# Softmax over 32768 columns on one core: eight equal column pieces per tile in place of five, and a finer cut of the last tile

## Chip, cores and metric

One core of a Trainium2 chip. The metric is the device time of one execution in microseconds, of the slowest core (here the only one). Executions of one kernel mostly agree within 0.3%. A run counts as slow when it lies more than 1.5% above the fastest of the same kernel; verdicts use the other runs, called fast here.

## The reference

```python
batch, seq, vocab = 16, 256, 32768          # logits: float32, temperature: 1.0
scaled = logits / temperature
scaled = scaled - scaled.max(axis=-1, keepdims=True)
exp_scaled = np.exp(scaled)
return exp_scaled / exp_scaled.sum(axis=-1, keepdims=True)
```

4096 rows of 32768 floats: 537 MB to read and 537 MB to write.

## The kernel before

Each row is cut into two halves that lie on neighbouring partitions, so there are 8192 half rows, 64 tiles of 128 half rows by 16384 columns (8.39 MB each). There are three tile buffers, of 64 KB per partition each. A tile is loaded, turned into probabilities in place, and stored from the same buffer. Loads go through the queue of the sync engine (SP), middle stores through that of ScalarE.

```python
_PIECES = (4096, 4096, 4096, 2048, 2048)
_ON_DVE = (4096, 4096, 2048, 0, 0)
_END = 4096                       # first and last tile: four pieces
_END_ON_DVE = 2560

def normalise(t):
    ...
    for k in range(K):            # one piece after the other
        nc.vector.tensor_reduce(out=nm[:, k:k+1], in_=xc, axis=X, op=A.max, negate=True)
        nc.scalar.activation(out=xc, in_=xc, func=Exp, bias=nm[:, k:k+1],
                             scale=inv_t, accum_out=ssum[:, k:k+1])
        if t == 1 and k == 0:
            store(0, 0, W)
    # max over pieces and over the two halves of a row; small exp `ee`; sum; reciprocal; factor f
    ...
    for k in range(K):            # scale: on_dve[k] columns on VectorE, the rest on ScalarE
        ...
        if t == G - 1:
            store(t, a, c)
    if 0 < t < G - 1:
        store(t, 0, W)

for t in range(_BUFS):
    load(t)
for t in range(G):
    normalise(t)
    if t and t + _BUFS - 1 < G:
        load(t + _BUFS - 1)       # waits until the store of tile t-1 is over
```

Each piece has a max of its own, so ScalarE can start its exp while VectorE looks at the next piece; the factors f put the pieces on one scale at the end.

## Time and profile before

| | kernel before |
|---|---|
| median of its first 3 runs | 2494.04 us (2493.56 to 2495.87) |
| span of the profiled run | 2496.7 us |
| VectorE (DVE) / ScalarE (ACT) busy | 63% / 55% |
| moved over the span | 430 GB/s |
| a middle tile: first max to store issue | 28.05 us |

In lines of a timeline the columns are the start in us, the length in us, engine, line of the kernel, operation, output <- input, shapes and the number of instructions that are merged; brackets give idle time before it and what ended that. In a table of stretches they are the stretch, its length, the busy time of each engine with its instruction count, the granted TensorE clock, the mean share of the 16 DMA engines, and GB/s. For the last two a packet is counted whole in the stretch in which it starts, so stretches of a few us show jumps that are not there. From the timeline of the kernel before:

```profile
1044.95 0.34 ACTq L70 DMA_DIRECT2D out_dram<-x  x1
1050.72 0.33 SPq L62 DMA_DIRECT2D x<-in_logits_dram  x1
```

The second line is the next load, issued once the store before this one has landed, 5.8 us later.

### The profile page before, as it was taken

What the parts mean: (1) busy time and instruction counts of PE and PEld (TensorE: products, weight loads), DVE (VectorE), ACT (ScalarE), POOL (GpSimd) and SP (SyncE); (2) the same over time, 40 slices, a digit from 0 to 9 for tenths busy, and PEclk for the clock granted to TensorE, in tenths of its full rate; (3) what the DMA queues carried; (4) which work ended last, traced back from release to release, by engine and by line L of the source; (5) the groups of instructions that cost most, each with busy time, mean ns of one, the idle gap of its engine ahead of it and who ended that gap; (6) DMA issues with size and microseconds to landing.
All of it is one profiled execution on the core that took longest, in us unless ns stands there. A gap on an engine that the chain in (4) does not pass through costs nothing.

```text
span 2496.7 us, 2616 instructions
## 1 busy us (share of the span) xinstructions
DVE 1575.6 (63%) x1216; ACT 1367.8 (55%) x895; POOL 0.2 (0%) x4
## 2 busy tenths in 40 slices
DVE  6576665766657656576565665656657566565665
ACT  6464654645546455464554645546455464554655
POOL 0000000000000000000000000000000000000000
DMA  9999999999999999999999999999999999999998
GB/s 419 436 429 430 433 437 436 435 437 426 434 434 437 433 426 435 434 436 423 433 433 433 435 425 436 436 433 425 435 422 436 421 437 436 421 436 422 436 429 380
DMA packets 19748, 1073.91 MB, mean 430 GB/s; under 512 B 2192, under 2 KB 2192, under 8 KB 2192
## 3 DMA queue, kind: packets, MB, share of 16 engines
q1 hardware_dynamic: 10800, 553.65, 51.4%
q10 hardware_dynamic: 8928, 520.10, 48.4%
q14 instruction: 20, 0.16, 0.0%
HBM read 536.87 MB, written 536.87 MB: 430 GB/s over the span
## 4 chain that ended last, share of the span: by engine, by line
DMA 73%; DVE 16%; ACT 9%; another core or an unknown queue 2%; issue 0%; SPq 0%; DVEq 0%; ACTq 0%
DMA x<-in_logits_dram 37%; DMA out_dram<-x 36%; DVE nm L101 12%; ACT x L108 7%; DVE x L140 3%; ACT x L144 2%; DVE f L136 0%; ACT ee L121 0%; DVE rS L135 0%; DVE Sh L80 0%; DVE ttj L124 0%; DVE Sh L77 0%; SPq L62 0%; DVEq L189 0%
## 5 line engine op out<-in xcount | busy, mean ns | idle before, releaser
L101 DVE TENSOR_REDUCE nm<-x 128x1 f32<-128x4096 f32 x318 | 1117.5, 3579 | 683.8 <-DMA x<-in_logits_dram 683.8
L108 ACT ACTIVATE x<-x,nm 128x4096 f32<-128x4096 f32 x318 | 965.4, 3036 | 1025.3 <-DVE nm L101 1025.3
L144 ACT ACTIVATE x<-x,f 128x2048 f32<-128x2048 f32 (+1 forms) x194 | 370.9, 1975 | 74.0 <-DVE f L136 74.0
L140 DVE TENSOR_SCALAR x<-x,f 128x4096 f32<-128x4096 f32 (+2 forms) x194 | 372.2, 1975 | 2.5 <-DVE f L136 0.2
L124 DVE CUSTOM_DVE_ANT_0 ttj<-ee,ssum 128x5 f32<-128x5 f32 (+1 forms) x64 | 10.6, 166 | 196.7 <-ACT ee L121 196.7
L108 ACT ACTIVATION_READ_ACCUMULATOR x<-x,nm 128x1 f32 x318 | 59.2, 186 | 0.0
L121 ACT ACTIVATE ee<-nm,nMh 128x5 f32<-128x5 f32 (+1 forms) x64 | 18.1, 284 | 0.0
L136 DVE TENSOR_SCALAR f<-ee,rS 128x5 f32<-128x5 f32 (+1 forms) x64 | 14.8, 231 | 2.2
L135 DVE RECIPROCAL rS<-Sh 128x1 f32<-128x1 f32 x64 | 10.5, 164 | 2.2
L80 DVE TENSOR_TENSOR Sh<-Sh 128x1 f32<-128x1 f32 x64 | 10.2, 159 | 2.2
L80 DVE TENSOR_TENSOR nMh<-nMh 128x1 f32<-128x1 f32 x64 | 10.2, 159 | 2.2
L119 DVE TENSOR_REDUCE nMh<-nm 128x1 f32<-128x5 f32 (+1 forms) x64 | 10.1, 158 | 2.2
L77 DVE STREAM_SHUFFLE Sh<-Sh 128x1 f32<-128x1 f32 x64 | 9.7, 151 | 0.0
L77 DVE STREAM_SHUFFLE nMh<-nMh 128x1 f32<-128x1 f32 x64 | 9.7, 151 | 0.0
L108 ACT ACT_TABLE_LOAD x1 | 1.3, 1283 | 8.1 <-DMA x<-in_logits_dram 8.1
L124 DVE DVE_READ_ACCUMULATOR2_ANT Sh<- 128x1 f32 x64 | 5.2, 82 | 0.0
L77 DVE LOAD_MASK_SELECT Sh<-Sh x64 | 0.9, 14 | 2.8
L77 DVE LOAD_MASK_SELECT nMh<-nMh x64 | 0.9, 14 | 2.8
L175 POOL MEMSET const-uint8-127<- 128x1 uint8 x1 | 0.1, 102 | 0.0
L175 POOL MEMSET const-bfloat16-1.0<- 128x1 bf16 x1 | 0.1, 101 | 0.0
L175 POOL MEMSET const-float32-0.0<- 128x1 f32 x1 | 0.1, 98 | 0.2 <-issue 0.2
L175 POOL MEMSET const-float32-1.0<- 128x1 f32 x1 | 0.1, 98 | 0.0
## 6 DMA issues: line engine op xcount, KB each, us to landing
x<-in_logits_dram SPq DMA_DIRECT2D x8, 2048.0 KB, 23.7
out_dram<-x SPq DMA_DIRECT2D x4, 2048.0 KB, 15.1
x<-in_logits_dram SPq DMA_DIRECT2D x62, 43.7
out_dram<-x ACTq DMA_DIRECT2D x62, 44.5
out_dram<-x SPq DMA_DIRECT2D x1, 29.4
```

Of the source, the lines that this page charges most:

```text
L77: nc.vector.stream_shuffle(out=v[:, j + 1 : j + 2], in_=v[:, j : j + 1], mask=mask)
L80: nc.vector.tensor_tensor(out=v[:, j + 1 : j + 2], in0=v[:, j : j + 1], in1=v[:, j + 1 : j + 2], op=op,)
L101: nc.vector.tensor_reduce(out=nm[:, k : k + 1], in_=xc, axis=X, op=A.max, negate=True)
L108: nc.scalar.activation(out=xc, in_=xc, func=Exp, bias=nm[:, k : k + 1], scale=inv_t, accum_out=ssum[:, k : k + 1],)
L119: nc.vector.tensor_reduce(out=nMh[:, 0:1], in_=nm, axis=X, op=A.min)
L121: nc.scalar.activation(out=ee, in_=nm, func=Exp, bias=nMh[:, n_rounds : n_rounds + 1], scale=-1.0)
L124: nc.vector.tensor_tensor_reduce(out=ttj, in0=ee, in1=ssum, scale=1.0, scalar=0.0, op0=A.mult, op1=A.add, accum_out=Sh[:, 0:1],)
L135: nc.vector.reciprocal(out=rS, in_=Sh[:, n_rounds : n_rounds + 1])
L136: nc.vector.tensor_scalar_mul(out=f, in0=ee, scalar1=rS)
L140: nc.vector.tensor_scalar_mul(out=xs[:, a:b], in0=xs[:, a:b], scalar1=f[:, k : k + 1])
L144: nc.scalar.activation(out=xs[:, b:c], in_=xs[:, b:c], func=Copy, scale=f[:, k : k + 1])
L175: nc = _bacc.Bacc("TRN2", target_bir_lowering=False, num_devices=1)
```

## The change

The intent: smaller, equal pieces let ScalarE keep up with VectorE, so that less is left after the last max and each store leaves earlier; in the last tile, smaller last pieces shorten the tail.

```diff
-_PIECES = (4096, 4096, 4096, 2048, 2048)
-_ON_DVE = (4096, 4096, 2048, 0, 0)
-_END = 4096
-_END_ON_DVE = 2560
+_PIECES = (2048, 2048, 2048, 2048, 2048, 2048, 2048, 2048)
+_ON_DVE = (2048, 2048, 2048, 2048, 2048, 0, 0, 0)
+_FIRST_PIECES = (4096, 4096, 4096, 4096)
+_FIRST_ON_DVE = (2560, 2560, 2560, 2560)
+_LAST_PIECES = (4096, 4096, 4096, 2048, 2048)
+_LAST_ON_DVE = (2560, 2560, 2560, 2048, 0)
 ...                              # load() and normalise() take their cut from cut(t)
-            if t == 1 and k == 0:
+            if t == 1 and k == 1:
                 store(0, 0, W)
```

More of the change, by code (lines that the diff above doesn't have):

```diff
@@ L10 @@
 _BUFS = 3
-_LOAD = 16384
-_PIECES = (4096, 4096, 4096, 2048, 2048)
-_ON_DVE = (4096, 4096, 2048, 0, 0)
-_END = 4096
-_END_ON_DVE = 2560
+_LOAD = (16384,)
+_PIECES = (2048, 2048, 2048, 2048, 2048, 2048, 2048, 2048)
[4 more added lines that the diff above has]
+_LAST_ON_DVE = (2560, 2560, 2560, 2048, 0)
 _SETS = 3
@@ L45 @@
     n_rounds = _SPLIT.bit_length() - 1
-    K = max(len(_PIECES), W // _END)
+    K = max(len(_FIRST_PIECES), len(_PIECES), len(_LAST_PIECES))
     pool = ctx.enter_context(tc.tile_pool(name="fixed", bufs=1))
@@ L57, with cut @@
     ]
+    def cut(t: int) -> tuple:
+        if t == 0:
+            return _FIRST_PIECES, _FIRST_ON_DVE, _FIRST_PIECES
+        if t == G - 1:
+            return _LAST_PIECES, _LAST_ON_DVE, _LAST_PIECES
+        return _PIECES, _ON_DVE, _LOAD
     def load(t: int) -> None:
-        n = _END if t in (0, G - 1) else _LOAD
-        for s in range(0, W, n):
+        s = 0
+        for n in cut(t)[2]:
             nc.sync.dma_start(
@@ L65, in load @@
             )
+            s += n
     def store(t: int, a: int, b: int) -> None:
@@ L88, in normalise @@
         xs = buf[t % _BUFS]
-        if t in (0, G - 1):
-            sizes = [_END] * (W // _END)
-            on_dve = [_END_ON_DVE] * len(sizes)
-        else:
-            sizes, on_dve = _PIECES, _ON_DVE
+        sizes, on_dve, _ = cut(t)
         K = len(sizes)
```

## The prediction

Its sum came to 0 in the middle, -1.1 us at the end for the DMA engines that don't set it and +1.6 for the one that does, +1 to +1.6 us in all, of which +1.0 was taken.

> **What bounds the kernel now.** I read the page of the kernel before from the top: the head, the 40 slices, the queues, the chain, the groups. Then the waits, the timeline of one middle tile and of the end, and a table of stretches over the end.
>
> ```profile
> DVE 1575.6 (63%) x1216; ACT 1367.8 (55%) x895; POOL 0.2 (0%) x4
> DMA  9999999999999999999999999999999999999998
> HBM read 536.87 MB, written 536.87 MB: 430 GB/s over the span
> DMA 73%; DVE 16%; ACT 9%; another core or an unknown queue 2%; issue 0%; SPq 0%; DVEq 0%; ACTq 0%
> L101 DVE TENSOR_REDUCE nm<-x 128x1 f32<-128x4096 f32 x318 | 1117.5, 3579 | 683.8 <-DMA x<-in_logits_dram 683.8
> ```
>
> Neither compute engine is the bound: VectorE is busy for 63% of the span and ScalarE for 55%, and VectorE's idle time (683.8 us) is waiting for loads. The transfers are at nine tenths or more in every slice but the last. Each tile is 128 rows of 16384 floats, 8.39 MB in and 8.39 MB out, and there are 64. The stretches confirm it:
>
> ```profile
> 800.00:1000.00 200.00, 125.79 (x106) 112.14 (x77) 0.00 (x0) 1.00 1.00 432
> 1000.00:1200.00 200.00, 128.56 (x100) 111.79 (x73) 0.00 (x0) 1.00 1.00 432
> ```
>
> The last two columns are the DMA share, 1.00, and 432 GB/s. At that rate a tile's 16.78 MB take 38.8 us, and that is the period at which tiles follow each other (first max at 1016.90, then at 1055.71). All 64 take 2485 us of the 2496.7 us span. So nothing that only shortens work on an engine can move the middle: the chain's 16% VectorE and 9% ScalarE are the way from a load to the store of the same tile, while another load and another store are in flight. What is left to win lies at the two ends, about 12 us together. The end:
>
> ```profile
> 2446.50:2469.70 23.20, 19.25 (x17) 16.15 (x11) 0.00 (x0) 1.00 1.00 429
> 2469.70:2471.70 2.00, 2.00 (x2) 2.00 (x2) 0.00 (x0) 1.00 0.15 66
> 2471.70:2491.40 19.70, 3.50 (x3) 3.42 (x3) 0.00 (x0) 1.00 1.00 425
> 2491.40:2495.10 3.70, 0.00 (x0) 0.00 (x0) 0.00 (x0) 1.00 0.06 27
> ```
>
> Three things are to be seen. Until 2469.7 the transfers are full. Then for 2.0 us they stand at a share of 0.15: the store before the last is drained on most of the 16 DMA engines and the last tile's first stored piece isn't there yet. From 2471.7 they are full again, and at 2491.4 fifteen engines are done. The share of 0.06 after it is one engine of sixteen (1/16 = 0.0625), which works alone at 27 GB/s for 3.7 us and sets the end. Individual DMA records agree: thirteen engines pause between 2469.7 and 2471.7, two go on to about 2472.2, and one still has two whole packets of the previous store to send, until 2475.6. That last one never pauses.
>
> [...] this trace holds 430 to 434[...]. [...] The queue part of this page has
>
> ```profile
> q14 instruction: 20, 0.16, 0.0%
> ```
>
> 20 packets, 0.16 MB, that is 8 KB each, for 2616 executed instructions: one packet for every 131. I read these as refills of the instruction streams. [...] here the max takes 4413 ns at 4096 and 2276 ns at 2048, so two halves cost 139 ns more than a whole, and the scaling 2350 and 1280, 210 ns more.
>
> **The change, part by part.** (a) Middle tiles, 62 of them, on VectorE: eight maxima of 2048 in place of three of 4096 and two of 2048: 8 x 2.276 - (3 x 4.413 + 2 x 2.276) = +0.42 us busy. Scaling: five of 2048 in place of two of 4096 and one of 2048: 5 x 1.280 - (2 x 2.350 + 1.280) = +0.42 us. Over 62 tiles +52 us: VectorE to about 1628 us. ScalarE: 8 x 1.985 - (3 x 3.708 + 2 x 1.985) = +0.79 us, and three more accumulator reads of 0.186; its three copies of 2048 stay. Over 62 tiles +83 us: ScalarE to about 1451 us. Both stay under 70% of the span, beside the transfers: zero on the path.
>
> (b) Way from load to store of a middle tile. This group's timeline shows it:
>
> ```profile
> 1016.90 17.46 DVE L101 TENSOR_REDUCE nm<-x 128x1 f32<-128x4096 f32 x5 [10.63 <-DMA x<-in_logits_dram]
> ...
> 1037.68 0.28 ACT L121 ACTIVATE ee<-nm,nMh 128x5 f32<-128x5 f32 x1
> ...
> 1039.06 5.81 DVE L140 TENSOR_SCALAR x<-x,f 128x4096 f32<-128x4096 f32 x3
> ```
>
> Now: the five maxima take 17.46 us with overlaps of about 0.07 each, and the small exp starts 20.78 us after the first, because ScalarE still has 4096-wide work queued. After: eight maxima at 2.21 are 17.7 us; ScalarE needs 1.98 per piece, less than 2.21, so it keeps up and the small exp starts about 2.0 later, at 19.7: 1.1 us earlier. The scaling then ends about 5 x 1.22 = 6.1 after its start in place of 5.81: 0.3 later. Net 0.8 us earlier per tile. In the middle this only makes a store wait longer in the queue: zero on the path.
>
> (c) The last two tiles, where VectorE does set the pace: the last tile's maxima start at 2446.58 with no idle time, straight after the scaling of the tile before, since its data had landed. The 0.8 us of tile 62 therefore moves the last tile forward. Inside the last tile, four maxima take 17.39 us and the small exp starts at 21.13 after the first; with 4096 three times and 2048 twice it is the old middle pattern, 20.78: 0.35 us earlier. The first stored piece has the same 2560 and 1536 columns. So the first of the last stores can be issued 1.1 us earlier, and the pause of 2.0 us shrinks to 0.9 for thirteen engines.
>
> (d) But the engine that ends last has no pause to shrink. Its end is the sum of its own transfers. Why it is behind: at the end 3.7 us, plus the 2.0 us pause that the others had, makes 5.7 us. An 8 KB packet at 27 GB/s takes 0.30 us, and 19 or 20 of them make 5.7 to 6.0 us. This is what it looks like if all refill packets run on this one engine; that is an estimate, not shown. The change adds instructions: VectorE 62 x (3 + 2) + 1 = 311; ScalarE 62 x (3 exps + 3 accumulator reads) + 2 = 374; one load and one store: some 687 in all, or 687/131 = 5.2 more packets. At 0.30 us each the last engine ends about 1.6 us later.
>
> (e) Start: tile 0 keeps its pieces. Its store is issued after the second piece of tile 1, which ends where the first 4096-wide one ended. Zero. Last stores in pieces of 1 MB: the same bytes, and the end is the straggler's last packet, so zero to within the 0.6 us of one packet.
>
> Sum: middle 0, end -1.1 for engines that don't set it, +1.6 for the one that does: about +1 to +1.6 us.
>
> **The rivals.** First, the refills are spread over several engines, or the straggler has another reason; then the end may follow the 1.1 us of (c) at most, and the time is about 2493. For it: a lag isn't proof of its cause. Against it: the sizes fit (5.7 against 20 x 0.30), and the straggler doesn't pause. Second, VectorE or ScalarE becomes the bound through eight pieces: it would take 38.8 us of work a tile on one engine; VectorE has about 26 a tile, ScalarE 23. Against it is everything; were it so, 2550 or more. Third, the changed phase between a store and the next load alters how well reads and writes share the engines. Most packets of 64 KB take 2.418 us, but some 560 in the middle take longer, by 195 us over 16 engines, or 12 us each; they come in bursts at hand-overs between stores. A shift of 0.8 us could add or remove a few us of this, in either direction: 2489 to 2500. Fourth, the intent of the change succeeds fully, the pause vanishes and the straggler with it: not more than 5 us, 2489.
>
> **Range and chances.** I take +1.0 us, between the straggler at +1.6 and the first rival at -1.1, weighted to the former: 2495.0 us. The three runs before span 2.3 us, and the third rival gives some 4 us either way: 2490.0 to 2499.5. A change by 2% is 50 us; the transfers forbid it on the fast side (12 us is all that isn't transfer), and on the slow side no engine is near enough. Faster 0.01, within 2% 0.98, slower 0.01.
>
> **What would show it.** Queue 14 with 25 or 26 packets and some 3300 instructions; 430 GB/s over the span and 1.00 in the middle; VectorE near 1628 and ScalarE near 1451 us; store issue in a middle tile some 27.2 us after its first max, against 28.05; the pause near 2470 cut to about 1 us; the time alone of the one engine at the end grown from 3.7 to over 5 us. I'd be wrong if that last stretch is as short as before or shorter, which undoes step (d); if a middle tile's share falls below 0.98, which means that the pieces reach the transfers after all; or if the period per tile departs from 38.8 us, which would be the third rival.

## More of the kernel before

The runs came in rounds. In the first measurement the kernel before was run 4 times; the four later rounds were on four different chips, each with the kernel before run 11 times beside the others. Every ratio is taken within its round.

## The result and the profile after

| | before | changed |
|---|---|---|
| median, first measurement | 2494.36 us (4 runs) | 2497.33 us (4 runs, one of them slow: 2536.12) |
| fast runs, first measurement | 1 | 1.0009 times before (95%: 0.9992 to 1.0027) |
| fast runs, second measurement | 1 | 1.0020 times before (0.9991 to 1.0049) |
| runs slow, both | 0 of 48 | 4 of 12 (2532 to 2536 us) |

Such a ratio is the mean time of one kernel's fast runs over that of the other's of the same rounds, so not quite the ratio of the medians. Over its 48 runs the kernel before lies between 2491.2 and 2504.6 us, which is the noise to bear in mind. The profile that came first fell into a slow run, so the changed kernel was run again unedited (the run "after_again" below) and the profile shown here is of a fast run of it.

The page of the changed kernel:

```profile
span 2500.1 us, 3305 instructions
DVE 1603.0 (64%) x1527; ACT 1454.2 (58%) x1269; POOL 0.2 (0%) x4
DMA  9999999999999999999999999999999999999998
HBM read 536.87 MB, written 536.87 MB: 429 GB/s over the span
q14 instruction: 26, 0.21, 0.0%
```

The engines are hardly nearer to being the bound, the transfers are as full as they were, and there are 26 packets on queue 14 in place of 20. These packets, of 8 KB each and of the kind that the page calls instruction, are called refill packets below. That they refill the instruction streams is the author's reading; what the pages show is that their number goes with the instructions: 20 for 2616, 26 for 3305, one for every 131 and 127. A middle tile in its timeline:

```profile
1018.03 17.64 DVE L107 TENSOR_REDUCE nm<-x 128x1 f32<-128x2048 f32 x8 [11.52 <-DMA x<-in_logits_dram]
...
1037.70 0.28 ACT L127 ACTIVATE ee<-nm,nMh 128x8 f32<-128x8 f32 x1
...
1039.08 6.07 DVE L146 TENSOR_SCALAR x<-x,f 128x2048 f32<-128x2048 f32 x5
...
1045.22 0.34 ACTq L80 DMA_DIRECT2D out_dram<-x  x1
```

The small exp starts 19.67 us after the first max (20.78 before), scaling takes 6.07 us (5.81 before), and the store is issued after 27.19 us, 0.86 us earlier. The intent is met, and nothing is won by it. The end, as a table of stretches:

```profile
2473.20:2475.40 2.20, 2.20 (x2) 2.20 (x2) 0.00 (x0) 1.00 0.25 104
2475.40:2495.10 19.70, 3.08 (x3) 3.87 (x3) 0.00 (x0) 1.00 0.99 416
2495.10:2498.70 3.60, 0.00 (x0) 0.00 (x0) 0.00 (x0) 1.00 0.07 27
```

The pause of most DMA engines is still there, 2.2 us against 2.0, and one engine alone ends after 3.6 us more, against 3.7. The whole end lies some 3.6 us later as it is (2469.7 to 2473.2, 2491.4 to 2495.1). So what this profile is longer by, it lost before the end; but a difference of 3.4 us between two single executions is within the noise.

**What the records of the transfers show.** Each DMA record of the trace has a start, a length and a queue. A row of a tile is one packet of 64 KB and nearly always takes 2.418 us. Where a new store starts, some of its first packets take longer: of the 16 first packets of the store issued at 1707.15 us in the kernel before, 13 take 2.9 to 3.5 us. In the table of stretches such a place shows only when rate and share are read together:

```profile
1709.00:1712.00 3.00, 0.00 (x0) 0.00 (x0) 0.00 (x0) 1.00 1.02 350
1712.00:1746.00 34.00, 24.61 (x19) 21.35 (x14) 0.00 (x0) 1.00 1.00 434
1721.00:1724.00 3.00, 3.00 (x2) 1.57 (x1) 0.00 (x0) 1.00 0.81 350
```

350 GB/s over 3 us is no dip in itself: the third stretch lies within the undisturbed second one and reads 350 too, because packets of 2.418 us fall unevenly into 3 us. But there the share falls with the rate, to 0.81. At 1709 the same bytes have a share of 1.02, because a packet that takes longer counts as busy for longer. A full DMA share was therefore not the proof that the middle can't lose, for which the prediction took it. Two measures from these records are used below. The spread is the time from the first of the 16 DMA engines that is done with a tile's transfer to the last one. The lead is the time from the issue of a store to the moment when the first engine is done with the transfer that ends next. Over the eleven profiles of fast runs with uncut middle transfers, tile by tile:

```
lead, us          0-1   1-2   2-2.5  2.5-3  3-3.5  3.5-4  over 4
tiles              13    32     51    127    293     63     60
lost per tile    0.05  0.45   0.55   0.29   0.05  0.001  0.003   (us per DMA engine, first packets over 2.418)
```

A store that is issued at least 3.5 us ahead loses next to nothing; with 1 to 2.5 us, about half a microsecond; below 1 us again little, in 13 tiles. This is a relation that was seen, not one that was set by hand.

The check of this document added one more sum from the same records: what all packets of 64 KB took beyond 2.418 us, over the whole execution, divided by 16. In the last table below it stands as "slow packets", beside the time of the profiled run. That time less this sum is 2484 to 2487 us in all eleven fast profiles, while the times range from 2490.6 to 2515.0. So to within 3 us, what separates these executions is packets that take longer, and not more pauses between them.

### The profile page after: what moved, and what is told of

Its sections match the earlier page's. It is cut to its first block, busy times and chain, and to the rows that moved or that the text cites. A ratio compares the mean times of both kernels' runs of the same rounds, so it can differ in the third digit from the quotient of the medians.

```text
span 2534.3 us, 3305 instructions
## 1 busy us (share of the span) xinstructions
DVE 1603.1 (63%) x1527; ACT 1454.2 (57%) x1269; POOL 0.2 (0%) x4
## 4 chain that ended last, share of the span: by engine, by line
DMA 74%; DVE 19%; ACT 4%; another core or an unknown queue 2%; issue 1%; SPq 0%; ACTq 0%
DMA x<-in_logits_dram 40%; DMA out_dram<-x 34%; DVE nm L107 15%; DVE x L146 3%; ACT x L114 2%; ACT x L150 2%; DVE f L142 0%; ACT ee L127 0%; DVE rS L141 0%; DVE Sh L90 0%; DVE ttj L130 0%; DVE Sh L87 0%; SPq L71 0%; ACTq L195 0%
## 5 line engine op out<-in xcount | busy, mean ns | idle before, releaser
L107 DVE TENSOR_REDUCE nm<-x 128x1 f32<-128x2048 f32 (+1 forms) x505 | 1128.6, 2309 | 775.6 <-DMA x<-in_logits_dram 775.6
L114 ACT ACTIVATE x<-x,nm 128x2048 f32<-128x2048 f32 (+1 forms) x505 | 1022.7, 2025 | 978.3 <-DVE nm L107 935.5
L146 DVE TENSOR_SCALAR x<-x,f 128x2048 f32<-128x2048 f32 (+1 forms) x318 | 387.9, 1289 | 2.3
L114 ACT ACTIVATION_READ_ACCUMULATOR x<-x,nm 128x1 f32 x505 | 94.2, 186 | 0.0
L130 DVE CUSTOM_DVE_ANT_0 ttj<-ee,ssum 128x8 f32<-128x8 f32 (+1 forms) x64 | 10.7, 167 | 116.2 <-ACT ee L127 116.2
L127 ACT ACTIVATE ee<-nm,nMh 128x8 f32<-128x8 f32 (+1 forms) x64 | 18.3, 285 | 0.0
L142 DVE TENSOR_SCALAR f<-ee,rS 128x8 f32<-128x8 f32 (+1 forms) x64 | 14.8, 231 | 2.2
L141 DVE RECIPROCAL rS<-Sh 128x1 f32<-128x1 f32 x64 | 10.5, 164 | 2.2
L125 DVE TENSOR_REDUCE nMh<-nm 128x1 f32<-128x8 f32 (+1 forms) x64 | 10.3, 161 | 2.2
L90 DVE TENSOR_TENSOR Sh<-Sh 128x1 f32<-128x1 f32 x64 | 10.2, 160 | 2.2
L90 DVE TENSOR_TENSOR nMh<-nMh 128x1 f32<-128x1 f32 x64 | 10.2, 159 | 2.2
## 6 DMA issues: line engine op xcount, KB each, us to landing
out_dram<-x SPq DMA_DIRECT2D x2, 1024.0 KB, 17.9
```

What stands on the lines that cost most here:

```text
L90: nc.vector.tensor_tensor(out=v[:, j + 1 : j + 2], in0=v[:, j : j + 1], in1=v[:, j + 1 : j + 2], op=op,)
L107: nc.vector.tensor_reduce(out=nm[:, k : k + 1], in_=xc, axis=X, op=A.max, negate=True)
L114: nc.scalar.activation(out=xc, in_=xc, func=Exp, bias=nm[:, k : k + 1], scale=inv_t, accum_out=ssum[:, k : k + 1],)
L125: nc.vector.tensor_reduce(out=nMh[:, 0:1], in_=nm, axis=X, op=A.min)
L127: nc.scalar.activation(out=ee, in_=nm, func=Exp, bias=nMh[:, n_rounds : n_rounds + 1], scale=-1.0)
L130: nc.vector.tensor_tensor_reduce(out=ttj, in0=ee, in1=ssum, scale=1.0, scalar=0.0, op0=A.mult, op1=A.add, accum_out=Sh[:, 0:1],)
```

## The experiments

Twelve runs were made, in the order below; the first is the changed kernel itself. All gave correct results.

**after_again**: the changed kernel, unedited.

> The changed kernel once more, unedited, to get a profile of its fast state and more times. Theory 1 (the straggling DMA engine sets the end, refill packets make it straggle): in a fast profile the middle holds 430 GB/s and more, and one engine works alone at the end for 4.5 to 6 us (before: 3.7), ratio of fast runs 1.000 to 1.002. Rival (the 1.1 us of earlier last stores reach the end): the lone stretch is as short as before and the ratio is 0.999 to 1.000. The slow state (2535 us in 2 of 6 runs so far) should come again in some of the runs if it belongs to this kernel: 1 to 3 of the 6.

Measured: 1.0020 (0.9991 to 1.0049), median 2507.83 us over six runs of which two are slow (2532.22 and 2535.31). The lone stretch at the end did not grow, so step (d) of the prediction fails in its size at least; the ratio, whose interval holds both 1.000 and 1.002, doesn't choose between the two.

**middle_only**: eight pieces in the middle, the last tile as before.

```diff
-_LAST_PIECES = (4096, 4096, 4096, 2048, 2048)
-_LAST_ON_DVE = (2560, 2560, 2560, 2048, 0)
+_LAST_PIECES = (4096, 4096, 4096, 4096)
+_LAST_ON_DVE = (2560, 2560, 2560, 2560)
```

> Eight pieces in the middle tiles, last tile as before. Theory 1: the instructions and so the refill packets are those of the changed kernel (26), so this one is about 1 to 2 us slower than the kernel before and equal to the changed kernel, and has slow runs as the changed kernel has. Rival (the last tile's pieces matter): it lies at least 0.5 us above the changed kernel.

Measured: 1.0021 (1.0002 to 1.0041), one slow run of 6 (2540.83). It has what the changed kernel has: a ratio as large, 26 refill packets.

**last_only**: middle tiles as before, the new last tile.

```diff
-_PIECES = (2048, 2048, 2048, 2048, 2048, 2048, 2048, 2048)
-_ON_DVE = (2048, 2048, 2048, 2048, 2048, 0, 0, 0)
+_PIECES = (4096, 4096, 4096, 2048, 2048)
+_ON_DVE = (4096, 4096, 2048, 0, 0)
-            if t == 1 and k == 1:
+            if t == 1 and k == 0:
```

> Middle as before, only the last tile in 4096, 4096, 4096, 2048, 2048. Theory 1: the last engine doesn't pause, so nothing is gained: ratio 1.000, within 0.5 us of the kernel before, 20 refill packets, the pause of the other engines near the end shorter by 0.3 us. Rival (the end follows VectorE): 0.3 us faster, which is below the noise of the times, so the profile has to decide. No slow runs if these come from the middle pieces.

Measured: 1.0003 (0.9987 to 1.0019), no slow run. The last tile's part of the change is worth nothing that can be measured, and what there is comes from the middle pieces.

**pool_refill**: the kernel before, with 2560 tiny memsets on the idle GpSimd.

```diff
+    idle = pool.tile([P, 1], fp32, tag="idle", name="idle")
     for t in range(G):
+        for _ in range(40):
+            nc.gpsimd.memset(idle, 0.0)
         normalise(t)
```

> The kernel before with 2560 one-column memsets on the idle GpSimd into a tile of their own that nobody reads: no added work on a busy engine, only some 2560/131 = 20 more refill packets, early in the run. Theory 1, if GpSimd's refills run on the same DMA engine: the straggler falls back by 20 x 0.3 = 6 us more, so the end comes up to 6 us later (2500), and slow runs may appear. Theory 1 with another DMA engine for GpSimd's refills: a second engine falls back by 6 us and the end stays within 2 us of before. Rival (refills cost nothing): 2494, nothing changes anywhere.

Measured: 1.0064 (1.0048 to 1.0080), 2510.88 us, no slow run: 16 us, where 6 were expected, and queue 14 has 41 packets. GpSimd runs its memsets in the first 440 us. Stretches of pool_refill:

```profile
100.00:300.00 200.00, 117.94 (x84) 99.41 (x63) 134.86 (x1128) 1.00 1.00 431
300.00:500.00 200.00, 120.34 (x95) 104.05 (x70) 106.89 (x876) 1.00 0.99 418
500.00:900.00 400.00, 251.00 (x197) 219.14 (x144) 0.00 (x0) 1.00 1.00 424
900.00:1300.00 400.00, 252.84 (x200) 221.62 (x148) 0.00 (x0) 1.00 1.00 433
```

The kernel before has 434, 435, 433 and 432 in these four stretches. So pool_refill has 431 and 418 GB/s while the refills come, still 424 for a while after (about half of the loss), then 433 as before. The spread of landings reads 12 us between 300 and 500 us, 10 up to 900 and 7 later. In the records a refill packet takes 0.309 us, and over the 20 refills of the kernel before the data packet of 64 KB that starts as a refill ends takes 0.12 to 0.62 us longer than 2.418, 0.39 at the mean; that is 0.70 us for one, not 0.30.

**pool_large**: the control, 280 memsets of 1024 columns in place of the 2560 tiny ones.

```diff
+    idle = pool.tile([P, 1024], fp32, tag="idle", name="idle")
+    for _ in range(280):
+        nc.gpsimd.memset(idle, 0.0)
     for t in range(G):
         normalise(t)
```

> Control for pool_refill: the kernel before with 280 memsets of 1024 columns on GpSimd, some 300 us of GpSimd work in the same part of the run, but only some 2 more refill packets in place of 20. If pool_refill lost its 16 us by refills: ratio 1.000 to 1.002 and no loss in the first 900 us. Rival (GpSimd's writes themselves disturb the transfers or VectorE): 1.005 or more, and the slow packets between 100 and 700 us come again.

Measured: 0.9995 (0.9976 to 1.0014), no slow run. GpSimd is busy for as long (306.8 us against 309.0), with 23 refill packets, and nothing is lost in the stretches in which it works:

```profile
100.00:300.00 200.00, 133.04 (x88) 103.54 (x67) 190.02 (x175) 1.00 1.01 434
300.00:500.00 200.00, 130.39 (x104) 111.27 (x75) 22.27 (x19) 1.00 1.00 434
```

Here GpSimd is done by about 320 us, so the first line is the one to read. So it isn't GpSimd's work that costs in pool_refill, it is its many instructions, close together. At this point the refill theory looked right.

**pieces_1024**: sixteen middle pieces.

```diff
-_PIECES = (2048, 2048, 2048, 2048, 2048, 2048, 2048, 2048)
-_ON_DVE = (2048, 2048, 2048, 2048, 2048, 0, 0, 0)
+_PIECES = (1024,) * 16
+_ON_DVE = (1024,) * 10 + (0,) * 6
-            if t == 1 and k == 1:
+            if t == 1 and k == 3:
```

> The changed kernel with sixteen middle pieces of 1024: per tile 13 more instructions on VectorE and 16 more on ScalarE than with eight, 62 tiles, so some 1800 more in all and 14 more refill packets (40), spread over the whole run; both engines stay far from full (VectorE near 70%). Refill theory: each refill costs about 0.7 us at the straggler as it did in pool_refill (16 us for 20), so 2494 + 20 x 0.7 = 2508, or the slow state near 2535 in most runs. Rival (the changed kernel's loss is only the way from load to store): within 0.1% of the changed kernel.

Measured: 1.0052 (1.0031 to 1.0072), 2509.34 us, 41 refill packets, no slow run. The number fits the refill theory's 2508 and is not a proof of it: in this kernel, too, the store leaves earlier than before, 27.6 us after the landing, so two causes move together.

**rows_halved**: the kernel before, each transfer cut into two of 64 rows.

```diff
+        H = P // 2
         for s in range(0, W, n):
-            nc.sync.dma_start(out=buf[t % _BUFS][:, s : s + n], in_=x[t * P : (t + 1) * P, s : s + n])
+            for r in (0, H):
+                nc.sync.dma_start(out=buf[t % _BUFS][r : r + H, s : s + n],
+                                  in_=x[t * P + r : t * P + r + H, s : s + n])
         # and the stores in the same way
```

> The kernel before with every load and store cut into two of 64 rows, packets still whole 64 KB rows. A half's load needs only the same half's store to be over, so the next load is queued some 15 us earlier and the other engines have work while one straggles. If the slow packets come from engines that run dry while the straggler holds the next issue back: they vanish (12 us per engine now), 2484 to 2489, ratio 0.996 to 0.998. Rival (the slow packets are the memory's own): 2494 and as many slow packets. The straggler's end itself stays.

Measured: median 3555.3 us, 1.4206 (1.4142 to 1.4270), one slow run of 6 (3587.88). A bad miss, which says nothing on the question:

```profile
HBM read 536.87 MB, written 536.87 MB: 304 GB/s over the span
```

The cause was not shown, and no run tested it. What the records show is that the packets of 64 KB of the loads took 4.4 us at the median in place of 2.418, and those of the stores 2.6.

**relief**: the loads of tiles 16 and 40 cut into 64, 60 and 4 rows, meant to spare one DMA engine.

```diff
+        if t in (16, 40):
+            for r, h in ((0, 64), (64, 60), (124, 4)):
+                nc.sync.dma_start(out=buf[t % _BUFS][r : r + h, :],
+                                  in_=x[t * P + r : t * P + r + h, :])
+            return
```

> The kernel before, but the loads of tiles 16 and 40 are cut into 64, 60 and 4 rows[...]. If the straggler is engine 15[...] the spread of landings falls at each and rises in between, and the time falls by 3 to 8 us (2486 to 2491). If the straggler is one of engines 0 to 3,[...] 2497 to 2500. If it is another, the time stays within 2 us of before.

It was the assumption that engine 15 is spared by the small cuts and that engines 0 to 3 get more to send; the forecasts rest on it.

Measured: 1.0256 (1.0229 to 1.0282), 2561.81 us. Another miss, and it looks like the one before: between 590 and 655 us, while the first of the two cut loads is under way, the load's packets of 64 KB take 4.4 us at the median and up to 9.7, the store's beside them 2.5. The second half of that time and what follows it, as a stretch:

```profile
634.00:680.00 46.00, 16.48 (x5) 10.98 (x5) 0.00 (x0) 1.00 0.98 346
```

Whether sparing the straggler helps is not answered by it, nor whether the cut spared any engine.

**store_late**: the kernel before, with a copy on ScalarE in front of each middle store.

```diff
+    idle = pool.tile([P, 2048], fp32, tag="idle", name="idle")
+    nc.gpsimd.memset(idle, 0.0)
         if 0 < t < G - 1:
+            nc.scalar.activation(out=idle, in_=idle, func=Copy, scale=1.0)
             store(t, 0, W)
```

> The kernel before with one copy of 2048 columns on ScalarE, in a tile of its own, in front of each middle store: the store is issued about 1.9 us later, with one instruction more per tile (half a refill packet in all). Over eight profiles so far, a tile loses 0.56 to 0.60 us per DMA engine where its store is issued less than 2.5 us before the first engine finishes the load in flight, 0.05 us at 3.0 to 3.5 and nothing above 3.5; the kernel before has 3.3 to 3.7 in most tiles. Lead theory: the lead falls below 2.5 in most tiles, 62 x 0.5 = some 30 us lost, 2515 to 2535. Rival (the transfers are the bound and a store only waits longer or shorter in its queue, as the prediction said): 2494 to 2497.

Measured: 0.9996 (0.9983 to 1.0010), 2494.84 us, no slow run. Read the timeline before reading this as a verdict:

```profile
1045.87 1.89 ACT L152 ACTIVATE idle<-idle 128x2048 f32<-128x2048 f32 x1
1046.01 0.34 ACTq L72 DMA_DIRECT2D out_dram<-x  x1
```

The store is issued 0.14 us after the copy began, not after it ended. It stands behind the copy in ScalarE's program, but it didn't wait for it. The copy went to another tile than the one stored; in after_held below, where it is on the stored data, the store is issued 0.03 us after the copy's end. The edit didn't do what it was meant to do, and the lead theory wasn't tested by it.

**same_count**: the kernel before with the changed kernel's instruction count: eleven tiny instructions per middle tile, behind the store.

```diff
+    idle_v = pool.tile([P, 1], fp32, tag="idle_v", name="idle_v")
+    idle_a = pool.tile([P, 1], fp32, tag="idle_a", name="idle_a")
+    nc.gpsimd.memset(idle_a, 0.0)
         if 0 < t < G - 1:
             store(t, 0, W)
+            for _ in range(5):
+                nc.vector.memset(idle_v, 0.0)
+            for _ in range(6):
+                nc.scalar.activation(out=idle_a, in_=idle_a, func=Copy, scale=1.0)
```

> The kernel before with its own pieces, and five one-column memsets on VectorE and six one-column copies on ScalarE per middle tile, in tiles of their own, behind the store: the instruction count of the changed kernel without its pieces. Refill theory: 25 or 26 refill packets, the straggler as far behind as with the changed kernel, and without its 0.8 us shorter way from load to store, so ratio 1.002 to 1.006, possibly slow runs near 2535. Rival (the piece sizes make the difference): 0.999 to 1.001.

Measured: 0.9994 (0.9980 to 1.0008), 2495.12 us, no slow run, with

```profile
q14 instruction: 26, 0.21, 0.0%
```

as in the changed kernel. The refill theory falls for this change: six more refills, spread over the run, cost nothing that can be measured (the interval ends at +0.08%). What the pieces do, and these instructions don't, is to send the store off earlier; here it left 28.05 us after the first max, as before.

**tapered**: a try at beating both kernels by an even earlier store at the old instruction count.

```diff
-_PIECES = (4096, 4096, 4096, 2048, 2048)
-_ON_DVE = (4096, 4096, 2048, 0, 0)
+_PIECES = (4096, 3584, 3328, 3072, 2304)
+_ON_DVE = (4096, 3584, 2560, 0, 0)
```

> A try at beating both: the kernel before with five middle pieces of 4096, 3584, 3328, 3072 and 2304 in place of 4096, 4096, 4096, 2048 and 2048, same instruction count. ScalarE then keeps up with VectorE and has less left after the last max: the small exp at about 20.2 us after the first max in place of 20.8, so each store is issued some 0.5 us earlier at the same refills. Lead theory: the loss of 0.05 to 0.2 us a tile shrinks, 2 to 8 us gained, ratio 0.997 to 0.999, slow packets below 6 us per engine (12 in the profile before). Rival: 1.000 within the noise.

Measured: 1.0027 (1.0011 to 1.0043), 2502.39 us, and one slow run of 6 (2551.68). The edit did what it was meant to do:

```profile
1020.22 17.46 DVE L101 TENSOR_REDUCE nm<-x 128x1 f32<-128x4096 f32 x5 [11.33 <-DMA x<-in_logits_dram]
...
1040.30 0.28 ACT L121 ACTIVATE ee<-nm,nMh 128x5 f32<-128x5 f32 x1
...
1047.56 0.34 ACTq L70 DMA_DIRECT2D out_dram<-x  x1
```

The store leaves after 27.34 us, 0.7 us earlier than before, with five pieces and 21 refill packets. It is slower all the same, and its interval lies clear of 1; slow packets are 15.2 us per engine where below 6 were expected. The expectation missed in its sign. That turned the theory round: an earlier store may be what costs.

**after_held**: the changed kernel, its store held back. The copy is in place this time, on data that the store sends, so that the store waits for it (issued at 1047.37 us, 0.03 us after the copy's end).

```diff
         if 0 < t < G - 1:
+            tail = xs[:, W - 1280 : W]
+            nc.scalar.activation(out=tail, in_=tail, func=Copy, scale=1.0)
             store(t, 0, W)
```

> The changed kernel, pieces and counts untouched, with one in-place copy of the tile's last 1280 columns (times 1.0, the values stay) on ScalarE in front of each middle store, so that the store must wait for it: from landing to store about 28.1 us again, as in the kernel before, in place of 27.2; one instruction more per tile. So far every kernel with 28.07 us lies at 2494 to 2497 with no slow run (before, last_only, pool_large, same_count, store_late, whose copy did not hold the store back), and every kernel with 27.2 to 27.6 us at 2500 or more, with slow runs in three of four (the changed kernel, middle_only, tapered, pieces_1024), whatever its refills. Theory of the way (an earlier store is what costs): back to 0.999 to 1.001 of the kernel before, no slow run in 6, slow packets below 13 us per engine. Rival (the small pieces themselves cost): 1.002 as before and one or two slow runs.

Measured: 0.9999 (0.9983 to 1.0016), 2496.21 us, no slow run of 6.

```profile
1019.14 17.64 DVE L107 TENSOR_REDUCE nm<-x 128x1 f32<-128x2048 f32 x8 [11.38 <-DMA x<-in_logits_dram]
...
1046.07 1.27 ACT L157 ACTIVATE x<-x 128x1280 f32<-128x1280 f32 x1
1047.37 0.34 ACTq L80 DMA_DIRECT2D out_dram<-x  x1
```

The eight maxima take their 17.64 us as in the changed kernel, the copy ends later than the scaling would have, and the store leaves 28.23 us after the first max. 62 copies more, and the kernel is back at the time of the kernel before. One reserve: this round ran on another chip than the rounds of the changed kernel, which wasn't run beside it, and the changed kernel's own intervals (1.0009, 1.0020) overlap with this one. The times alone don't show the way back; the spread does, at 7.3 us in place of 10.5.

**All of them in one table**, from the profiles of fast runs: the median time from a load's landing to the issue of its tile's store, the time from that to the next load's issue, the median spread between 1000 and 2400 us, refill packets, slow packets and the time of the profiled run, ratio and slow runs.

| kernel | landing to store | store to next load | spread | refills | slow packets, us | profiled run, us | ratio of fast runs | slow runs |
|---|---|---|---|---|---|---|---|---|
| before | 28.07 | 5.79 | 7.5 | 20 | 13.5 | 2498.45 | 1 | 0 of 48 |
| last_only | 28.07 | 5.77 | 7.3 | 21 | 6.6 | 2490.56 | 1.0003 | 0 of 6 |
| pool_large | 28.07 | 5.66 | 7.3 | 23 | 8.5 | 2493.42 | 0.9995 | 0 of 6 |
| store_late | 28.07 | 5.75 | 7.3 | 21 | 9.9 | 2494.84 | 0.9996 | 0 of 5 |
| same_count | 28.07 | 5.71 | 7.3 | 26 | 11.1 | 2495.10 | 0.9994 | 0 of 6 |
| after_held | 28.26 | 5.54 | 7.3 | 26 | 13.1 | 2497.28 | 0.9999 | 0 of 6 |
| pool_refill | 28.07 | 5.79 | 7.1 | 41 | 21.5 | 2508.17 | 1.0064 | 0 of 6 |
| changed | 27.22 | 6.67 | 10.5 | 26 | 16.3 | 2501.91 | 1.0009, 1.0020 | 4 of 12 |
| middle_only | 27.22 | 6.82 | 10.2 | 26 | 17.9 | 2502.74 | 1.0021 | 1 of 6 |
| tapered | 27.37 | 6.61 | 9.2 | 21 | 15.2 | 2500.72 | 1.0027 | 1 of 6 |
| pieces_1024 | 27.59 | 6.46 | 10.0 | 41 | 28.1 | 2515.04 | 1.0052 | 0 of 6 |

The kernels fall into two groups, and the first column sorts them; refills and number of pieces don't. The second column moves against the first, so which of the two intervals matters was not taken apart. With 28 us the spread is 7 to 7.5 us, with 27.2 to 27.6 it is 9 to 10.5, whatever else differs. pool_refill stands apart: it has the long way, and loses its time in the stretch where its refills come in a rush and just after it. pieces_1024 has both the short way and 41 refills, and loses most of the second group; which of the two its extra 0.25% over tapered is due to was not taken apart.

Slow packets follow the ratio only roughly: before and last_only have the same middle, and 13.5 and 6.6 us. What one execution has of them seems to be as much chance as kernel; the spread is steadier.

No kernel that was run beats the kernel before.

## Why the prediction was right, and where its steps were not

The outcome was as predicted: within 2%, and the median of 2497.33 us (2497.90, 2496.76 and 2493.43 in its fast runs) lies in the range of 2490.0 to 2499.5. The reason given first holds: the transfers are the bound, at 429 to 430 GB/s in both kernels, and a gain by over 2% was shut out. What it drew from a share of 1.00 at 432 GB/s, that nothing that only shortens work on an engine can move the middle, was too much: the kernel before has 13.5 us of slow packets in its own profile, more than most of these kernels differ by. The +1.0 us that it settled on owes its place to luck, since neither of the terms that it was weighed from came true (steps (c) and (d)).

- Step (a), engine work: ScalarE was predicted at 1451 us and measured at 1454. VectorE was predicted at 1628 and measured at 1603, because one instruction's start overlaps the one before: eight maxima take 17.64 us in the timeline (eight times their mean of 2.277 us is 18.2), 0.18 more than five, not 0.42. Off the path in either case.
- Step (b), the way from load to store: 0.8 us earlier was predicted, 0.86 measured. "In the middle this only makes a store wait longer in the queue: zero on the path" is the sentence that failed. It isn't zero, and its sign is against the change: tapered has little else than an earlier store and is slower by 0.27%, and after_held takes the earliness away from the changed kernel and stands at 0.9999, with the spread back from 10.5 to 7.3 us. The changed kernel's own two intervals reach below 1, so a loss of about 0.1 to 0.2% is not established by itself; it is read from middle_only (1.0002 to 1.0041) and tapered.
- Step (c), the pause of thirteen engines near the end: predicted to shrink from 2.0 to 0.9 us, measured at 2.2. The order within the last tiles moved as worked out (the last tile's small exp at 20.77 us after its first max, as predicted), and the last tile's first piece was ready 51.8 us after the first max of the tile before it, in place of 53.0, about the 1.1 us foreseen. But the store before it was drained earlier as well, after 49.6 us in place of 51.0, so the pause stayed. last_only, which has part (c) of the last tile alone, is at 1.0003.
- Step (d), the straggler: the count of refill packets was right (25 or 26 predicted, 26 found), their cost (0.30 us) was not: 0.70 us with the longer packet behind them. That all of them run on one DMA engine is probably wrong as well: in the fast profile of middle_only two refills of 0.31 us start within 0.18 us of each other (78.5 and 78.7 us), so they overlap. And the lone stretch at the end, predicted at over 5 us, stayed at 3.6, which is the sign that the prediction itself named for undoing this step. The lag is no running sum of refills either. From the moment at which the other engines are done to the last packet:

```profile
2489.80:2491.70 1.90, 0.00 (x0) 0.00 (x0) 0.00 (x0) 1.00 0.06 26
2501.30:2504.70 3.40, 0.00 (x0) 0.00 (x0) 0.00 (x0) 1.00 0.16 67
```

  The first line is same_count with 26 refill packets, the second pool_refill with 41, against 3.7 us with 20 in the kernel before; over the eleven fast profiles it is 1.9 to 3.9 us, in no order of refills. In pool_refill the spread even falls back from 12 to 7 us. The +1.6 us of this step came out near the size of the real loss for a wrong reason: same_count has all the refills and none of the loss.
- The rivals: the third, that a changed phase between a store and the next transfer alters how well the engines are used, comes nearest to what was found, and the prediction gave it 4 us in either direction. Its range was kept by this rival's width. The second, an engine as bound, is refuted by 64% and 58% busy. The first and fourth, gains of 1 to 5 us, did not come.

What stays open: why an earlier store makes it worse. Seen is that it goes with a wider spread of the DMA engines over a transfer (10 us against 7), and that stores with a short lead lose time in their first packets (0.45 to 0.55 us per DMA engine at 1 to 2.5 us). But the mean lead of the changed kernel in the profile (3.3 us over 57 tiles) is hardly below that of the kernel before (3.5), and pool_large has a lower one (3.1) and no loss. With 15 tiles of 57 under 2.5 us against 4, the relation is one of the tail: such tiles are 2 to 7 in the kernels with the long way (10 in pool_refill) and 10 to 24 in those with the short one. What makes the slow state, which came in 6 of 30 runs of kernels with the short way and in none of 35 with the long way (nor in 48 of the kernel before), wasn't examined; the rounds were on different chips, and the last one, with after_held, had no kernel with the short way in it.

## What to carry to other kernels

Where transfers are the bound, as here, shortening the compute between a load and its store isn't sure to be free: it shifts when a store joins the queue, and here kernels in which it came 0.7 to 0.9 us earlier ran 0.1 to 0.3% longer. A DMA share of 1.00 doesn't prove that nothing can be lost there, because packets that take longer count as busy (1709 to 1712 us: 1.02 at 350 GB/s, with first packets of 2.9 to 3.5 us in place of 2.418), and a steady rate doesn't prove it either (the kernel before holds 430 to 435 GB/s in each stretch of 200 to 400 us between 100 and 2400 us, with 13.5 us of slow packets per DMA engine in the run); look at the length of single packets and at how far apart the DMA engines end a transfer. And when an instruction is added as a delay, see in the timeline that it delays: in store_late the store left 0.14 us after the start of a copy of 1.89 us that stood in front of it in the program.
